# Neighbourhood and context probabilities as half-precision planes transposed by DMA, in a two-layer hybrid attention kernel on one core

## The chip, the core and the metric

The kernel runs on one core of one Trainium2 chip. The metric is the device time of one execution in microseconds (us), as the median over several runs. A core has a matrix engine (TensorE, "PE" in the profile, with its weight loads as "PEld"), a vector engine (VectorE, "DVE"), a scalar engine (ScalarE, "ACT"), a general one (GpSimd, "POOL") and a queue engine (SyncE, "SP") that here only issues DMA transfers. Each engine runs its own instructions in the order of its program and waits on semaphores. Sixteen DMA engines move data between memories.

## The reference

Two layers of a diffusion backbone. Each layer modulates and normalises 512 latent and 256 context tokens of width 1024, projects them once to the queries, keys, values and gates of two token mixers, and merges these. Mixer A is neighbourhood attention on an 8 x 64 grid with 8 heads of 64 (a window of 8 x 16 and a learned bias), whose latent queries also read all context keys. Mixer B is grouped-query attention, 8 query heads on 2 key heads. In the first layer the context is updated too, and its queries read only context keys.

```python
def _na_latent(q, k, v, kc, vc, rpb, rows):
    ...
        s_win = jnp.einsum('bchd,bicjhd->bhcij', qr, kw).astype(jnp.float32) * scale + bias[None]
        s_ctx = jnp.einsum('bchd,blhd->bhcl', qr, kc).astype(jnp.float32) * scale
        s = jnp.concatenate([s_win.reshape(B, NA_HEADS, GRID_W, wr * WIN_C), s_ctx], axis=-1)
        p = jax.nn.softmax(s, axis=-1).astype(v.dtype)
        ...
        return (jnp.einsum('bhcij,bicjhd->bchd', p_win, vw)
                + jnp.einsum('bhcl,blhd->bchd', p_ctx, vc))
...
def _layer(x, ctx, ...):
    hx = _rmsnorm(x, norm_g) * (1.0 + scale_x) + shift_x
    hc = _rmsnorm(ctx, norm_g) * (1.0 + scale_c) + shift_c
    px = hx @ w_in
    a_k, a_v, b_k, b_v, a_q, b_q, a_z, b_z, g_a, g_b = _split(px, SPLIT_SIZES)
    ...
    a_att = _na_latent(qa, ka, va, cka, cva, rpb, rows)
    ...
    b_att = _gqa_latent(qb, k_all, v_all)
    out_x = _merge(a_att, b_att, a_z, b_z, g_a, g_b, w_o_a, w_o_b, w_out)
    x_new = x + gate_x * out_x
    if update_ctx:
        c_a_att = _attend(cqa, cka, cva).reshape(B, L, NA_WIDTH)
        ...
        ctx = ctx + gate_c * out_c
    return x_new, ctx
```

## The kernel before

All is computed to single precision. Each large product is made of three products of split operands: a rounded high part (a 32-bit type with fewer mantissa bits, written `R(...)` in the code) and the remainder, `hi*hi + hi*lo + lo*hi` (`mm3`, L427 to L431). A weight tile is loaded from DRAM on SP's queue (`raw`, three buffers), rounded by ACT (`whi`), and its remainder is taken by DVE or POOL (`wlo`; L391 to L418).

A layer runs in stages. The latent and context rows are projected to keys, values and queries of mixer A; then comes the neighbourhood stage; then the projections of mixer B; then the grouped-query stage; then the output projections. In both attention stages `pipeline` (L993) goes over the eight heads: scores of head h, then the values of head h - 1, then a share of `fill`, which holds matmuls of other projections (gates and output) together with their weight loads. So TensorE has work beside the attention. The order in which each engine's program stands is made by a scheduler at build time; it may move instructions among one another within their dependences.

The neighbourhood stage, per head:

- `na_scores` (L934): four query blocks of 128. Block 0 holds the two edges of the grid, 64 queries each; blocks 1 to 3 hold the rest. Scores go to PSUM (L857, L858, L951), DVE adds the bias table and finds the maximum (L954), ACT takes the exponential and the sum (L957) into a tile `p` of 128 queries x 512 keys in 32 bits. `softmax_tail` (L756) normalises `p`: on DVE for blocks 0 and 2 (L761), on POOL for 1 and 3 (L763, L764). The bias tables `bint` and `bedg` have one buffer each and are loaded per head (L928).
- `ctx_scores` (L863), in layer 0 alone: 256 context queries on 256 context keys, in two blocks of 128.
- `na_values` (L964): `transpose_split` (L767) transposes 128x128 blocks of `p` on TensorE into PSUM (L773, L775), four blocks a call and four calls a head; ACT rounds the result to `pth` (L781) and DVE takes the remainder `ptl` (L782). Then TensorE multiplies them with the values, kept in two tiles `va` as high and low parts (L977 to L988). `ctx_values` (L884) does the same with one call for the context (L896 to L902).
- `head_out` (L785) adds the two halves of the result and multiplies it into `za`, the gate path's tile.

The grouped-query stage already has another form. Its probabilities are not normalised at first; `turned` (L795) writes them as two planes of 16-bit floats, ACT the rounded plane (L798) and DVE or POOL the remainder (L799), and a transposing DMA, issued on SP, writes them into `ht` (L800). `gq_values` (L1133) multiplies `ht` with values that are scaled to use the range of 16-bit floats (`shrink`, L811, and `split_vb`, L1068), as a high and a low part (and the high part once more), and `divide` (L802) applies the sums and the scale afterwards. The context's probabilities of this stage take the same way into `ct` (in the profile also under the name `vb`, the tile whose spare columns hold every other one).

The adaptive gates: `ada_steps` (L276) computes dot products on DVE in the background of other stages; at their end `ada_gate` (L310) writes 16 (layer 0) or 8 (layer 1) rows of 128 factors to DRAM (`gd`), straight from a tile that holds them as 128 rows of 16 or 8 (L317). They are read back, spread over all partitions, before the last projection (`gv`, L1180).

Large tiles of 128 x 3072 words come from a pool of nine (`big`, L89).

```python
pt = psw(512, "s" if att["spare"] and att["turn"] % 2 else "t")
...
        T.transpose(pt[:, c0:c0 + 128], src, ident)
...
S.copy(hi[:, n0:n1], pt[:, n0:n1])
V.tensor_tensor(lo[:, n0:n1], pt[:, n0:n1], F(hi[:, n0:n1]), ALU.subtract)
```

Of the kernel before, what the change touches and what calls it, by code (L numbers as in the profile page):

```python
# [25 lines left out]
NP_NA = (7, 8)  # L26
# [3 lines left out]
NT_NA = 2  # L30
# [20 lines left out]
def R(ap):  # L51
    return ap.bitcast(F32R)
# [18 lines left out]
def hybrid_kernel(es: ExitStack, tc, x, ctx, cvec, w_ada, w_ada0, small, gvec, w_in, w_o_a, w_o_b, w_out,  # L71
# [238 lines left out]
    def ada_gate(l, nv):  # L310
# [6 lines left out]
        nc.sync.dma_start(gd[l][0:n].rearrange("n p -> p n"), g[:, 0:nv].rearrange("p v k -> p (v k)"))  # L317
# [232 lines left out]
    def split_v(ps, hi, lo, hi_src=None):  # L550
        S.copy(R(hi), ps)
        V.tensor_tensor(R(lo), ps, hi, ALU.subtract)

    def evac_va(dsts):
        def f(t, ps):
            d = dsts[t // 3].rearrange("p (t n) -> p t n", t=3)[:, t % 3, :]
            d = d.rearrange("p (r q d) -> p r q d", q=4, d=64)
            s = ps.rearrange("p (r e d) -> p r e d", e=2, d=64)
            hi, lo = d[:, :, 0:4:3, :], d[:, :, 1:3, :]
            split_v(s, hi, lo)  # L560
        return f
# [18 lines left out]
    def layer(l, hx, nxt, start):  # L580
# [8 lines left out]
        def gate_steps(halves, pool):  # L589
            return (ada_steps(l, range(16, 24), halves, nv, pool)  # L590
                    + ([lambda: ada_gate(l, nv)] if 1 in halves else []))
# [133 lines left out]
        va = [big("va0"), big("va1")]  # L725
        w = load_w(W, C_AV, 512, KT, mix_lo)
        for t in range(6):
            tok_proj(w, 512, a_hx, t, evac_va(va))
# [26 lines left out]
        if True:  # L755
            def softmax_tail(p, n, r, pieces, eng=None):  # L756

                V.reciprocal(r, r)
                for i, (c0, c1) in enumerate(pieces):
                    if eng is None:  # L760
                        V.tensor_scalar(p[:, c0:c1], p[:, c0:c1], r[:, i:i + 1], 0.5, ALU.mult, ALU.mult)  # L761
                    else:
                        G.tensor_scalar(r[:, i:i + 1], r[:, i:i + 1], 0.5, None, ALU.mult)  # L763
                        G.tensor_tensor(p[:, c0:c1], p[:, c0:c1],  # L764
                                        r[:, i:i + 1].to_broadcast([128, c1 - c0]), ALU.mult)

            def transpose_split(blocks, n0=0, n1=512):  # L767

                att["turn"] += 1
                pt = psw(512, "s" if att["spare"] and att["turn"] % 2 else "t")  # L770
                for src, c0 in blocks:
                    if c0 is None:
                        T.transpose(pt.rearrange("p (s n) -> p s n", n=64)[:, 0:8:7, :], src, ident)  # L773
                    else:
                        T.transpose(pt[:, c0:c0 + 128], src, ident)  # L775
                if att["spare"]:
                    hi, lo = R(p_tile()[:, 0:512]), R(p_tile()[:, 0:512])
                else:
                    hi = att["p"].tile([128, 512], F32R, tag="pth", name=nm("pth"), bufs=att["nt"])
                    lo = att["p"].tile([128, 512], F32R, tag="ptl", name=nm("ptl"), bufs=att["nt"])  # L780
                S.copy(hi[:, n0:n1], pt[:, n0:n1])  # L781
                V.tensor_tensor(lo[:, n0:n1], pt[:, n0:n1], F(hi[:, n0:n1]), ALU.subtract)  # L782
                return hi, lo

            def head_out(po, e, dst, eng=None):  # L785
# [5 lines left out]
                S.copy(a, po[o:o + 64, :n])  # L791
                V.tensor_tensor(a, po[m:m + 64, :n], a, ALU.add)
                (eng or G).tensor_tensor(dst, dst, a, ALU.mult)

            def turned(p, n, out, eng):  # L795

                h = att["p"].tile([128, 2, n], F16, tag="h", name=nm("h"), bufs=att["nh"])
                S.copy(h[:, 0], p[:, :n])  # L798
                eng.tensor_tensor(h[:, 1], p[:, :n], h[:, 0], ALU.subtract)  # L799
                nc.sync.dma_start_transpose(out, h.rearrange("p a n -> p (a n)"))  # L800
# [9 lines left out]

            def shrink(v, s, mx, row):  # L811

                V.tensor_reduce(mx[:, 0:1], v, AX, ALU.max)
                V.tensor_reduce(mx[:, 1:2], v, AX, ALU.min, negate=True)
                V.tensor_tensor(mx[:, 0:1], mx[:, 0:1], mx[:, 1:2], ALU.max)
                pt = psw(512, "t")
                T.transpose(pt[0:1, 0:128], mx[:, 0:1], ident)
                V.tensor_reduce(row[:, 0:1], pt[0:1, 0:128], AX, ALU.max)
                T.matmul(pt[:, 128:129], row[:, 0:1].to_broadcast([1, 128]), ident[0:1, 0:1], start=True, stop=True)
                V.tensor_scalar(s[:, 1:2], pt[:, 128:129], 1.0e-30, 1.0 / V_UP, ALU.max, ALU.mult)  # L820
                V.reciprocal(s[:, 0:1], s[:, 1:2])
                V.tensor_scalar(s[:, 1:2], s[:, 1:2], 0.5, None, ALU.mult)
# [673 lines left out]
```

## Time and profile before

| | |
|---|---|
| median of 3 runs | 1131.86 us (1130.71 to 1135.87) |
| the profiled execution | 1136.54 us, span 1134.8 us, granted clock 0.989 |
| neighbourhood stage, layer 0 | about 150 to 305 us |
| grouped-query stage, layer 0 | about 384 to 507 us |
| neighbourhood stage, layer 1 | about 783 to 893 us |
| grouped-query stage, layer 1 | about 955 to 1066 us |
| DMA moved | 161.29 MB in 195278 packets |

All lines are of one profiled execution; times are from its first instruction. "Busy" of PE is modelled, since matmuls overlap: the start times in the timeline tell what one costs. In a group's row stand the line of the code, the engine, the operation, the tiles (out<-in), shape and count, then busy us and mean ns, then the idle time of the engine just before and what ended it. A row of a source line has the least, median and largest duration in ns. In the timeline a row has start, duration, engine (SPq: the queue of SP), line, operation and tiles; the idle time before it and its releaser stand in brackets.

### The profile page before, as it was taken

Reading aid. Unit: us, or ns where it says so; the run is one execution under the profiler, and the core shown is the slowest. Engines: PE = TensorE matmul, PEld = TensorE weight load, DVE = VectorE, ACT = ScalarE, POOL = GpSimd, SP = SyncE. Lnnn points to the kernel's source line nnn. Section 1 sums busy time; section 2 is a strip of 40 time slices with the busy share of each in tenths; the row PEclk is TensorE's granted clock in tenths of the full one; section 3 lists DMA queues with packets and bytes.
Section 4 is the critical chain, followed back from the end, with each engine's and each line's share of the span. In section 5 each row is a group of like instructions: output and inputs, shape, how many; then the busy total and the mean of one; then the engine's idle time right before and its main releaser. Section 6 shows DMA issues by size and latency. Waiting matters only on the chain.

```text
span 1134.8 us, 16867 instructions
## 1 busy us (share of the span) xinstructions
PE 1092.4 (96%) x5824; PEld 905.5 (80%) x5824; DVE 765.3 (67%) x1492; ACT 578.0 (51%) x1152; POOL 490.5 (43%) x405
## 2 busy tenths in 40 slices
PE   8999999999999999779999999999999999999998
PEld 5688888888988877557788888887888987777677
DVE  4666788888365478636567895357988765677473
ACT  6463266656333566555331275325666545776431
POOL 1044255654246245345521454335554563463530
PEclk9999999999999999989999999999999999999999
DMA  9454412233341597679733542453333236989742
GB/s 366 148 173 134 126 49 66 83 125 98 110 140 47 130 205 176 108 216 248 192 104 127 158 149 77 142 182 72 108 105 112 64 103 164 186 219 250 198 147 81
DMA packets 195278, 161.29 MB, mean 142 GB/s; under 512 B 119444, under 2 KB 161144, under 8 KB 193528
## 3 DMA queue, kind: packets, MB, share of 16 engines
q1 hardware_dynamic: 187856, 145.82, 47.2%
q0 software_dynamic: 2368, 7.87, 2.1%
q10 hardware_dynamic: 4968, 6.53, 1.7%
q8 instruction: 46, 0.75, 0.3%
q14 instruction: 40, 0.33, 0.1%
HBM read 115.58 MB, written 17.32 MB: 117 GB/s over the span
## 4 chain that ended last, share of the span: by engine, by line
PE 78%; DMA 6%; DVE 5%; issue 5%; POOL 3%; ACT 2%; SPq 1%; POOLq 0%; ACTq 0%; DVEq 0%
PE psx L431 11%; PE psx L430 11%; PE psx L429 11%; PE psf L429 9%; PE psf L430 8%; PE psf L431 8%; PE pst L775 2%; PE pss L951 2%; PE pss L857 2%; PE pss L858 2%; DMA raw<-in_w_in_dram 2%; DMA ht<-h 1%; PE pst L521 1%; PE pst L1144 1%; PE pst L1145 1%
## 5 line engine op out<-in xcount | busy, mean ns | idle before, releaser
L429 PE MATMUL psf<-hx,whi 128*128 128x512 f32 (+1 forms) x360 | 137.9, 383 | 4.1 <-ACT zt L610 2.5
L416 POOL TENSOR_TENSOR wlo<-raw,whi 128x512 fp32r<-128x512 f32 x70 | 98.0, 1405 | 94.4 <-ACT whi L414 64.3
L431 PE MATMUL psf<-hx,wlo 128*128 128x512 f32 (+1 forms) x360 | 135.8, 377 | 0.0
L430 PE MATMUL psf<-hx,whi 128*128 128x512 f32 (+1 forms) x360 | 135.2, 376 | 0.0
L429 PE MATMUL psx<-whi,hx 128*128 128x512 f32 (+1 forms) x328 | 120.7, 371 | 0.0
L430 PE MATMUL psx<-wlo,hx 128*128 128x512 f32 (+1 forms) x328 | 119.7, 366 | 0.0
L431 PE MATMUL psx<-whi,hx 128*128 128x512 f32 (+1 forms) x328 | 119.5, 365 | 0.0
L414 ACT CAST whi<-raw 128x512 fp32r<-128x512 f32 x136 | 82.5, 620 | 72.6 <-DMA raw<-in_w_in_dram 44.9
L402 POOL TENSOR_TENSOR wlo<-raw,whi 128x512 fp32r<-128x512 f32 x40 | 61.0, 1528 | 120.6 <-ACT whi L399 73.0
L799 POOL TENSOR_TENSOR h<-p,h 128x768 f16<-128x768 f32 (+1 forms) x40 | 64.9, 1626 | 99.7 <-ACT h L798 79.1
L399 ACT CAST whi<-raw 128x512 fp32r<-128x512 f32 x88 | 54.4, 623 | 100.4 <-PE psx L431 33.9
L500 POOL TENSOR_TENSOR ss<-ss,ehalf 128x8 f32<-128x8 f32 (+2 forms) x40 | 62.2, 1558 | 74.1 <-DVE ss L497 74.0
L416 DVE TENSOR_TENSOR wlo<-raw,whi 128x512 fp32r<-128x512 f32 x66 | 66.6, 1009 | 28.9 <-ACT whi L414 27.4
L1127 DVE CUSTOM_DVE_ANT_0 p<-pss,vb 128x768 f32<-128x768 f32 x64 | 60.2, 953 | 36.7 <-PE pss L858 19.9
L429 PEld LDWEIGHTS psf<-hx,whi 128*128 128x128 f32 x360 | 67.9, 189 | 16.1 <-ACT zt L610 3.6
L431 PEld LDWEIGHTS psf<-hx,wlo 128*128 128x128 f32 x360 | 67.8, 188 | 11.5
L430 PEld LDWEIGHTS psf<-hx,whi 128*128 128x128 f32 x360 | 67.9, 189 | 10.3
L1128 ACT ACTIVATE p<-pss,mx 128x768 f32<-128x768 f32 x64 | 57.5, 900 | 35.0 <-DVE mx L1127 31.5
L431 PEld LDWEIGHTS psx<-whi,hx 128*128 128x128 f32 x328 | 61.9, 189 | 10.0
L430 PEld LDWEIGHTS psx<-wlo,hx 128*128 128x128 f32 x328 | 62.0, 189 | 9.2
L429 PEld LDWEIGHTS psx<-whi,hx 128*128 128x128 f32 x328 | 61.7, 189 | 8.9
L429 PE MATMUL psx<-hx,whi 128*128 128x256 f32 (+1 forms) x208 | 68.1, 327 | 0.0
(359 smaller groups left out, 3097.5 us busy)
## 6 DMA issues: line engine op xcount, KB each, us to landing
raw<-in_w_in_dram SPq DMA_DIRECT2D x168, 256.0 KB, 2.9
rawb<-in_w_ada_dram SPq DMA_DIRECT2D x48, 256.0 KB, 2.8
raw<-in_w_out_dram SPq DMA_DIRECT2D x32, 256.0 KB, 3.1
tg<-gs SPq DMA_DIRECT2D x4, 1536.0 KB, 6.4
rawx<-in_w_ada_dram SPq DMA_DIRECT2D x4, 1024.0 KB, 13.3
rawy<-in_w_ada_dram SPq DMA_DIRECT2D x4, 1024.0 KB, 10.3
gs<-zt ACTq DMA_DIRECT2D x16, 256.0 KB, 2.1
raw<-in_w_o_a_dram SPq DMA_DIRECT2D x16, 256.0 KB, 3.4
```

The lines of the kernel that those rows point to most:

```text
L399: S.copy(hi[:, :n], raw[:, :n])
L402: e.tensor_tensor(lo[:, :n], raw[:, :n], F(hi[:, :n]), ALU.subtract)
L414: S.copy(hi, raw)
L416: lo_eng(i).tensor_tensor(lo, raw, F(hi), ALU.subtract)
L429: T.matmul(ps, lhs[0], rhs[0], start=first, stop=False)
L430: T.matmul(ps, lhs[0], rhs[1], start=False, stop=False)
L431: T.matmul(ps, lhs[1], rhs[0], start=False, stop=last)
L500: G.tensor_tensor(ss, ss, ehalf[:, :n], ALU.pow)
L775: T.transpose(pt[:, c0:c0 + 128], src, ident)
L799: eng.tensor_tensor(h[:, 1], p[:, :n], h[:, 0], ALU.subtract)
L1127: V.tensor_tensor_reduce(p, pss, lift, -1.0, 3e38, ALU.add, ALU.min, mx[:, 0:1])
L1128: S.activation(p, pss, AF.Exp, bias=mx[:, 0:1], accum_out=r[:, i:i + 1])
```

## The change

In the neighbourhood stage the probabilities too go through `turned` and a transposing DMA. `turned` gets the sums `r`: it forms the reciprocal, times 2^14, and on DVE's blocks (0 and 2) applies it while it writes the two 16-bit planes (ACT the rounded one, DVE the remainder in one fused operation); on POOL's blocks (1 and 3) POOL multiplies `p` by it first, ACT rounds and POOL takes the remainder. The DMA writes 128 transposed columns of `ht` per block; block 0 goes as two DMAs of 64 partitions each, to the two edges. The context's probabilities of layer 0 go the same way, one DMA a head, with DVE for the remainder.

The values `va` become pairs of 16-bit floats, scaled by the largest value over all tokens: each token tile is copied in 32 bits (`vf`), ACT takes absolute values and DVE their maximum (`size`), and after the first query tile `split_va` finds the largest over the partitions (a transpose and a small matmul on TensorE) and writes the pairs in three steps. The scale is taken back in `head_out`. The values of mixer B are held as pairs too, without the second high part. `transpose_split` and `softmax_tail` are gone.

`na_values` has four matmuls of 512 columns, four of 192 and eight of 128 per head, all on 16-bit operands; the two middle token tiles, which were one range of 256 columns, are now two of 128, since each query block's columns lie in their own plane. In `ctx_values` four of 256 columns stay.

`ht` has two places: part of one more large tile (`spare`) for even heads, a tile of the stage's pool for odd ones; `spare` holds the context's planes too. The number of `p` tiles goes from 7 and 8 to 3 and 4 (layers 0 and 1), `h` tiles are 3 and 4; tiles `r` go from 8 to 4.

`ada_gate` transposes its tile on TensorE, copies the rows out of PSUM on ACT and stores them as rows.

Instruction counts of the program: matmuls and transposes 5764 to 5546, transposing DMAs 72 to 160, other DMAs on SP 411 in both, POOL's two-operand operations 328 to 360, those of DVE 564 to 454.

```diff
-NP_NA = (7, 8)
+NP_NA = (3, 4)
+NH_NA = (3, 4)
-NT_NA = 2
+P_UP = 2.0 ** 14
...
-        nc.sync.dma_start(gd[l][0:n].rearrange("n p -> p n"), g[:, 0:nv].rearrange("p v k -> p (v k)"))
+        pt = psw(512, "t")
+        T.transpose(pt[0:n, 0:128], g[:, 0:nv].rearrange("p v k -> p (v k)"), ident)
+        gt = pool.tile([16, 128], F32, tag="agt", name=nm("agt"), bufs=1)
+        S.copy(gt[0:n], pt[0:n, 0:128])
+        nc.sync.dma_start(gd[l][0:n], gt[0:n])
...
+    def size(v, junk, mx):
+
+        S.activation(junk, v, AF.Abs)
+        V.tensor_reduce(mx, junk, AX, ALU.max)
+
+    def halves(v, d, s):
+
+        S.activation(d[:, :, 0, :], v, AF.Copy, scale=s)
+        V.scalar_tensor_tensor(d[:, :, 1, :], v, s, d[:, :, 0, :], ALU.mult, ALU.subtract)
...
+        def evac_va(t, ps):
+            S.copy(vf[:, t, :], ps)
+            size(ps, vab[:, 512 * t:512 * t + 512], vmx[:, t:t + 1])
+
+        def split_va():
+            V.tensor_reduce(vmx[:, 6:7], vmx[:, 0:6], AX, ALU.max)
+            shrink(vmx[:, 6:7], vsa, vsa[0:1, 2:3], 0.5 / P_UP)
+            for t in range(0, 6, 2):
+                halves(vf[:, t:t + 2, :].rearrange("p t (h d) -> p (t h) d", d=64),
+                       va[:, t:t + 2].rearrange("p t h q d -> p (t h) q d"), vsa[:, 0:1])
...
             tok_proj(w, 512, a_hx, t, evac_na(qav, True, gq, YB if first else 4))
+            if t == 0:
+                split_va()
...
-            def turned(p, n, out, eng):
+            def turned(p, n, out, eng, r=None):
 
                 h = att["p"].tile([128, 2, n], F16, tag="h", name=nm("h"), bufs=att["nh"])
-                S.copy(h[:, 0], p[:, :n])
-                eng.tensor_tensor(h[:, 1], p[:, :n], h[:, 0], ALU.subtract)
-                nc.sync.dma_start_transpose(out, h.rearrange("p a n -> p (a n)"))
+                if r is not None:
+                    V.reciprocal(r, r)
+                    eng.tensor_scalar(r, r, P_UP, None, ALU.mult)
+                    w = n // r.shape[-1]
+                if r is None or eng is G:
+                    if r is not None:
+                        G.tensor_tensor(p, p, r.to_broadcast([128, n]), ALU.mult)
+                    S.copy(h[:, 0], p[:, :n])
+                    eng.tensor_tensor(h[:, 1], p[:, :n], h[:, 0], ALU.subtract)
+                else:
+                    for i in range(n // w):
+                        c = slice(w * i, w * i + w)
+                        S.activation(h[:, 0, c], p[:, c], AF.Copy, scale=r[:, i:i + 1])
+                        V.scalar_tensor_tensor(h[:, 1, c], p[:, c], r[:, i:i + 1], h[:, 0, c], ALU.mult, ALU.subtract)
+                for o, (n0, n1) in out:
+                    nc.sync.dma_start_transpose(o, h[n0:n1].rearrange("p a n -> p (a n)"))
...
-                    softmax_tail(p, 512, r[:, 0:1], [(0, 512)], G if i in NA_POOL else None)
-                    ps_.append(p)
+                    at = [(0, 64, 0), (448, 512, 64)] if i == 0 else [(128 * i - 64, 128 * i + 64, 0)]
+                    turned(p, 512, [(ht[:, :, a:b], (n, n + b - a)) for a, b, n in at],
+                           G if i in NA_POOL else V, r[:, 0:1])
...
-                po = psw(512, "s" if h == 6 else "v")
+                    return va[:, t, h].rearrange("p q d -> p (q d)")
+                po = psw(512, "t")
                 for k in range(2):
...
-                    T.matmul(po, vsl(4 + k), hi, start=k == 0, stop=False)
-                    T.matmul(po, vsl(4 + k), lo, start=False, stop=False)
...
+                    for a in range(2):
+                        T.matmul(po, vsl(4 + k), ht[:, 4 * a + 2 + k, :], start=k + a == 0, stop=False)
+                for t, part in enumerate((((0, 192, 0),), ((64, 192, 1), (192, 320, 0)),
+                                          ((192, 320, 1), (320, 448, 0)), ((320, 512, 1),))):
+                    for n0, n1, k in part:
+                        for a in range(2):
+                            T.matmul(po[:, n0:n1], vsl(t), ht[:, 4 * a + k, n0:n1], start=False,
+                                     stop=t == 3 and a == 1)
```

More of the change, by code (lines that the diff above doesn't have):

```diff
@@ L755, in layer, with head_out @@
         if True:
[L756 to L785, printed above, removed]
+            def head_out(po, e, dst, eng=None, back=None):
                 n = dst.shape[-1]
@@ L1018, in na_first, with values_of @@
                 q = stage_q(qav[:, j, :], e)
[L1019 to L1022 removed]
+                st = na_scores(h, q, kh, kl)
+                if not first:
+                    return st, None
+                o = 4096 + 1024 * (h % 2)
+                ct = spare[:, o:o + 1024].rearrange("p (a i k n) -> p a i k n", a=2, i=2, k=2)
+                return st, ctx_scores(q, kh, kl, ct, False)
+            def values_of(dst, f, back, late):
                 def g(h, st):
```

158 lines of the change are left out of this document (61 added, 97 removed).

## The prediction

> **What bounds the kernel now.** I read the page's header first, then the busy time of each engine by stage, then the instruction timeline of TensorE around every hole, then the timeline of SP's queue.
>
> ```profile
> span 1134.8 us, 16867 instructions
> PE 1092.4 (96%) x5824; PEld 905.5 (80%) x5824; DVE 765.3 (67%) x1492; ACT 578.0 (51%) x1152; POOL 490.5 (43%) x405
> ```
>
> TensorE has no holes for 96% of the span, so its work is the time, plus its few holes. By stage (columns: stretch, its length, busy us of PE, weight loads, DVE, ACT, POOL, then granted clock, DMA share, GB/s; the rows are neighbourhood attention of layer 0, grouped-query attention of layer 0, and the same two of layer 1):
>
> ```profile
> 150.00:305.00 155.00, 155.00 (x971) 138.38 (x970) 121.36 (x272) 93.02 (x212) 75.29 (x74) 1.00 0.28 87
> 384.00:507.00 123.00, 104.23 (x601) 84.72 (x599) 81.78 (x154) 77.67 (x151) 49.54 (x36) 0.96 0.78 165
> 783.00:893.00 110.00, 108.54 (x598) 93.24 (x599) 92.97 (x186) 73.94 (x155) 57.66 (x56) 1.00 0.34 102
> 955.00:1066.00 111.00, 105.31 (x499) 79.43 (x498) 77.23 (x122) 77.33 (x138) 61.29 (x42) 1.00 0.98 219
> ```
>
> Both neighbourhood stages are bound by TensorE alone, with the DMA engines two thirds idle. The grouped-query stages already transpose by DMA: there the DMA share is 0.78 and 0.98, and TensorE is idle 18.8 and 5.7 us. Most of the 18.8 is one hole:
>
> ```profile
> 486.71 0.59 PE L1144 MATMUL pst<-ht,vb 128*128 128x512 f16 x1 [11.83 <-DMA ht<-h]
> 489.60 0.38 PE L1145 MATMUL pst<-ht,vb 128*128 128x512 f16 x1
> ...
> 464.93 0.37 SPq L317 DMA_DIRECT2D gd<-ag  x1
> ...
> 467.89 16.43 SPq L800 DMA_TRANSPOSE ht<-h  x3
> ...
> 468.00:476.00 8.00, 6.88 (x48) 6.22 (x46) 6.71 (x12) 4.42 (x10) 2.89 (x3) 1.00 0.18 9
> 480.00:488.00 8.00, 1.29 (x4) 0.49 (x5) 1.93 (x3) 4.34 (x8) 1.54 (x2) 0.50 1.08 234
> ```
>
> The gate store at 464.93 writes 2048 separate 4-byte values. Behind it SP's queue stands: three transposes take 16.43 us to issue, the DMA engines move 9 GB/s for 8 us, and TensorE waits 11.83 us for a transposed tile. The clock then stands at 0.50.
>
> **1. Transposes leave TensorE.** By the code a head has 16 transposes of 128x128 (L773, L775), and in layer 0 four more for the context: 16 x 16 + 8 x 4 = 288.
>
> ```profile
> L775 PE MATMUL pst<-ident,p 128*128 128x128 f32 x212 | 35.3, 272 | 0.0
> L773 PE MATMUL pst<-ident,p 128*128 128x128 f32 x60 | 16.0, 272 | 0.0
> ...
> 183.83 0.27 PE L773 MATMUL pst<-ident,p 128*128 128x128 f32 x1
> 183.93 0.49 PE L775 MATMUL pst<-ident,p 128*128 128x128 f32 x3
> 184.26 0.27 PE L773 MATMUL pst<-ident,p 128*128 128x128 f32 x1
> 184.37 0.49 PE L775 MATMUL pst<-ident,p 128*128 128x128 f32 x3
> 184.62 0.47 PE L429 MATMUL psf<-hx,whi 128*128 128x512 f32 x1
> 184.93 0.39 PE L430 MATMUL psf<-hx,whi 128*128 128x512 f32 x1
> 185.16 0.40 PE L431 MATMUL psf<-hx,wlo 128*128 128x512 f32 x1
> ```
>
> One lasts 272 ns, but they overlap: four go from 183.83 to 184.26, so 0.11 us each from start to start. The next four and a 512-column matmul take 0.67 us up to 184.93, and that matmul alone 0.23 (184.93 to 185.16): again 0.11. I take the spacing: 288 x 0.11 = 31.7 us off the path.
>
> The Trainium skill ("TensorE: Matmul & The Clock Gate", Part 4: PE-mode transpose) puts a transpose at about 275 ns in a kernel. The duration here agrees; by it the gain would be 79 us, but the start times decide.
>
> **2. Value matmuls.** Before, a head has four of 512 columns at 0.23, then eight of 192 or 256. After, four of 512, four of 192 and eight of 128, in half precision.
>
> ```profile
> 1013.76 0.38 PE L1145 MATMUL pst<-ht,vb 128*128 128x512 f16 x1
> 1013.98 0.38 PE L1144 MATMUL pst<-ht,vb 128*128 128x512 f16 x1
> ...
> 156.84 0.22 PE L857 MATMUL pss<-kh,qs 128*128 128x128 f32 x1
> 156.90 0.28 PE L858 MATMUL pss<-kl,qs 128*128 128x128 f32 x1
> 157.02 0.39 PE L857 MATMUL pss<-kh,qs 128*128 128x384 f32 x1
> ```
>
> Half precision goes at 0.22 per 512 columns. By columns alone a head takes 4 x 0.22 + 4 x 0.083 + 8 x 0.055 = 1.65 us after, and 4 x 0.23 + 4 x 0.086 + 4 x 0.115 = 1.72 before. But the second 128-column matmul above takes 0.12 to the next one's start (156.90 to 157.02), the first 0.06. At 0.12 for all eight a head takes 2.17. So -1 to +7 us over 16 heads; I take 0, since the two rows lie on both sides of 0.055 to 0.12. The largest value of V and the gate rows add, over both layers, four transposes and two tiny matmuls: 0.6 us, 1 with their waits (bounds 0 and 3); projection matmuls stand around each and hide them, and without that cover each shows its DVE reduction, about 0.7.
>
> **3. The gate store.** Rows go out as 16 descriptors of 512 bytes. In layer 0 this gives back the hole and the slow clock after it: seven matmuls go from 486.71 to 489.60 in 2.9 us instead of 7 x 0.22, 1.4 us more. 11.8 + 1.4 = 13.2 us. In layer 1 the same store holds weight loads:
>
> ```profile
> 767.69 0.38 SPq L317 DMA_DIRECT2D gd<-ag  x1
> ...
> 772.23 12.04 SPq L411 DMA_DIRECT2D raw<-in_w_in_dram  x4
> ...
> 784.02 0.50 PE L429 MATMUL psf<-hx,whi 128*128 128x512 f32 x1 [1.61 <-DVE za L612]
> ```
>
> There 1.6 us, bounds 0 and 2. What is late next is what is late already: of layer 0's 18.8 us without the 11.8, 7 us are other small holes, and I leave them as they are.
>
> **4. What it adds to DMA and SP.** Per head three full transposes (128x1024) and two of 64 partitions; in layer 0 one more for the context. That is 88 more issues on SP, whose queue also carries weight loads and bias tables.
>
> ```profile
> L800 SPq DMA_TRANSPOSE ht<-h x64: 1273/1594/12456, 388.6 to 1060.1; - x64
> L800 SPq DMA_TRANSPOSE ct<-h x4: 1232/1426/2273, 418.4 to 551.0; - x4
> ht<-h SPq DMA_TRANSPOSE x64, 4.3
> ...
> 789.94 0.89 SPq L411 DMA_DIRECT2D raw<-in_w_in_dram  x2
> 791.01 0.34 SPq L929 DMA_DIRECT2D bint<-in_bias_int_dram  x1
> 791.62 1.11 SPq L931 DMA_DIRECT2D bedg<-in_bias_edge_dram  x2
> ...
> 871.25 0.38 SPq L929 DMA_DIRECT2D bint<-in_bias_int_dram  x1
> ```
>
> Engine time: layer 1's two attention stages have similar loads, and 32 transposes of 128x1536 lift the share from 0.34 of 110 us to 0.98 of 111. So (108.8 - 37.4) / 32 = 2.2 us each, 1.5 for 128x1024. Four equivalents a head in layer 1 add 48 us to 37: 85 of some 95 us, 0.9. Layer 0: five a head, 60 + 43 = 103 of some 137, 0.75.
>
> Queue time in layer 1: a head lasts (871.25 - 791.01) / 6 = 13.4 us; without its transposes 11.6. SP issues five transposes at 1.43 or less (7.1), bias 1.45, four weight loads at 0.45 (1.8) and a spill taken at the bias load's 0.34: 10.7 of 11.6 us. That is tight. In the changed program's order TensorE reads a head's transposed tiles only after the next head's scores, about a head of matmuls later, so some 11 us cover the 4.3 us landing. The bias table has one buffer: SP waits for a head's last score row before it reloads it, and the transposes and weight loads stand behind that wait; before, only weight loads did. If the queue slips further, the cover is gone: each late weight load holds ACT's rounding, then POOL's remainder, then TensorE.
>
> **5. Vector engines.**
>
> ```profile
> L782 DVE TENSOR_TENSOR ptl<-pst,pth 128x512 fp32r<-128x512 f32 x35 | 23.5, 682 | 3.2 <-ACT pth L781 3.0
> L761 DVE TENSOR_SCALAR p<-p,r 128x512 f32<-128x512 f32 x32 | 23.8, 744 | 0.7
> L1074 DVE SCALAR_TENSOR_TENSOR vb<-vf,vb 128x768 f16<-128x768 f32 x2 | 2.4, 1224 | 1.7 <-ACT vb L1072 1.7
> L799 POOL TENSOR_TENSOR h<-p,h 128x512 f16<-128x512 f32 x8 | 9.8, 1219 | 16.3 <-ACT h L798 11.6 <-issue 4.7
> ```
>
> DVE loses four subtractions (2.6) and two scalings (1.5) a head and gains two fused ones at 1224 x 512/768 = 0.82, two tiny ones: -2 us a head. POOL gains two subtractions, 2.4 us a head: in layer 1 57.7 + 19.5 = 77 of 95. ACT stays, save six absolute values and three wide roundings of V per layer, hidden by the projections' matmuls (uncovered, the last three with their remainders are 3 x 1224 x 1024/768 = 4.9 us a layer). All of it hides while TensorE runs, but layer 1 then has every engine and the DMA at 0.8 to 0.9. For new waits, bounds from the stages above: none (layer 0's neighbourhood stage now has 155.00 of 155), or two to three times what the grouped-query stage shows (5.7 us idle of 111 at share 0.98). I take 3 us in layer 0 (0 to 15) and 8 in layer 1 (0 to 20), nearer the grouped-query row as share and chain are alike.
>
> **Sum.** -31.7 + 0 + 1 - 13.2 - 1.6 + 11 = -34.5 us against the profiled execution, whose own time is 1136.54 (span 1134.8 and 1.7 around it), 4.7 above the median of 1131.86. 1131.9 - 34.5 = 1097 us.
>
> **Rivals.**
>
> A (0.61): as summed, from 1085 (no new wait, value matmuls at -1) to 1110 (25 us of waits and slow small matmuls).
>
> B (0.19): the transposing queue sets layer 1's pace. Then its neighbourhood stage keeps its 110 us, losing its 14 us of the 31.7, and layer 0 loses half of its 17.6: 1131.9 - 14.8 - 8.8 + 1 = 1109, to 1128 where layer 0 and the small matmuls give back more. For: 0.98 share in its twin. Against: TensorE still ran 105 of 111 there. The Trainium skill ("DMA: Bandwidth & Descriptors", Specifications) wants 512 bytes or more for line rate, which speaks against many small transposing packets; the 0.98 share at 219 GB/s agrees.
>
> C (0.07), slower: every head exposes one transpose to TensorE, because its remainder comes last on POOL and SP then takes it behind weight loads whose buffer is not free. Price: issue 1.6 + landing 4.3 = 5.9 us, 16 heads, 94 us against the 46.5 won: 1131.9 + 1 + 94 - 46.5 = 1180. It decides from 2.9 us a head. Against: the head of matmuls in between, by the order above.
>
> D (0.10): the store is not what stands in SP's queue; the hole comes back behind other transposes: 1097 + 13 = 1110.
>
> E (0.03): transposes cost TensorE their whole 272 ns: 47 us more, 1050.
>
> **Numbers.** Forecast 1097. The range 1083 to 1123 holds A, D and most of B; it leaves out C, E and B's end. No change means within 0.5% (5.7 us), about what a measurement can tell. Faster takes A, D, E and B but its end: 0.88; same 0.05; slower 0.07.
>
> **What would show it.** TensorE's records fall by some 220 and spacing elsewhere stays; no hole over 3 us near the gate store, whose followers issue in about 1.5 us; neighbourhood stages near 140 and 100 us, DMA shares near 0.75 and 0.9. Holes at the value matmuls waiting for ht say C; at weight rounding waiting for raw loads, B. Wrong altogether if either neighbourhood stage is longer than now.

## The result: slightly slower, and the profile after

| | before | after |
|---|---|---|
| median | 1132.52 us (1130.71 to 1135.87, 7 runs) | 1138.45 us (1136.35 to 1139.72, 7 runs) |
| ratio to before, 95% interval | | 1.0049 [1.0036, 1.0062] |
| the profiled execution, its span, granted clock | 1136.54, 1134.8, 0.989 | 1139.45, 1137.6, 0.980 |

The forecast was 1097 us; the change costs 5.9 us instead, 0.5%, with an interval that is clear of no change. The head of the page after:

```profile
span 1137.6 us, 16739 instructions
PE 1075.8 (95%) x5608; PEld 872.4 (77%) x5608; DVE 780.9 (69%) x1472; ACT 603.7 (53%) x1180; POOL 535.1 (47%) x437
```

TensorE has 216 records fewer, as foreseen, yet DVE and POOL are both busier than before. By stage (same columns as in the prediction: stretch, length, busy us of PE, weight loads, DVE, ACT, POOL, then clock, DMA share, GB/s; neighbourhood and grouped-query stage of layer 0, then of layer 1):

```profile
150.00:302.00 152.00, 136.90 (x790) 113.14 (x789) 126.32 (x254) 100.22 (x216) 96.03 (x89) 0.94 0.69 151
407.00:555.00 148.00, 131.18 (x719) 102.18 (x720) 102.95 (x177) 90.02 (x173) 68.25 (x50) 0.97 0.84 193
790.00:898.00 108.00, 96.56 (x494) 75.75 (x493) 84.31 (x164) 73.01 (x146) 78.50 (x70) 0.94 0.78 176
973.00:1073.00 100.00, 95.69 (x454) 70.20 (x452) 66.94 (x107) 67.42 (x120) 57.63 (x39) 1.00 0.92 218
```

Layer 0's neighbourhood stage had TensorE busy for 155.00 of 155 us; now it is idle for 15.1 of 152, with a granted clock of 0.94. The stages' lengths alone mislead: the scheduler moved projection matmuls out of the neighbourhood stages into the stretches behind them. So I compare each stage with the TensorE work that lies in it, and for the stages before I take the stretches that hold the same part of the program. They differ from the prediction's in two places (layer 0's grouped-query and layer 1's neighbourhood stage, before):

```profile
401.00:558.00 157.00, 134.04 (x730) 105.78 (x731) 98.81 (x179) 89.86 (x174) 68.98 (x50) 0.93 0.78 182
779.00:891.00 112.00, 110.00 (x599) 93.85 (x597) 94.42 (x186) 73.80 (x153) 57.97 (x57) 1.00 0.35 105
```

Work is the number of matmuls of each shape times the spacing at which that shape starts when nothing holds it (0.2275 us for 512 columns in 32 bits, 0.2165 in 16 bits, and so on); *lost* is the rest of the stage. It holds idle time and slow clock, and the choice of the spacings moves it by about 1 us a stage.

| lost, us | before | after |
|---|---|---|
| neighbourhood, layer 0 | 1.2 | 26.0 |
| grouped query, layer 0 | 31.8 | 23.9 |
| neighbourhood, layer 1 | 4.2 | 20.4 |
| all else | 26 | 28 |
| whole span | 63 | 98 |
| TensorE work in the whole span | 1072 | 1040 |

The work fell by 32 us, which the prediction had as 31.7. Counted without these spacings, as TensorE's busy time less half of what lay at half clock, it fell from 1085.1 to 1058.6 us, so by 26.5. The losses rose by 35. So the gain was earned and given back in the two neighbourhood stages, +25 and +16. What TensorE waited for there, after (engine, tile and line, releaser: us in total, times, longest; layer 0 first, then layer 1):

```profile
PE pst L971 <- DMA ht<-h: 4.0, 4, 1.3
PE psv L894 <- DMA ht<-h: 3.5, 2, 1.9
PE psv L894 <- DVE r L803: 3.0, 1, 3.0
PE psf L434 <- DVE zt L624: 2.2, 2, 1.8
...
PE pss L861 <- DVE mx L951: 5.4, 3, 2.3
PE psx L434 <- DVE mx L951: 2.9, 1, 2.9
PE pss L948 <- DVE mx L951: 2.1, 2, 1.5
```

In layer 1 nearly all of it is DVE: mostly PSUM tiles of scores that DVE has not emptied yet. In layer 0 half is transposed tiles that land late, and these are written by DVE or POOL before the transfer.

**Why DVE is late.** Groups of instructions on DVE in layer 0's neighbourhood stage, first after, then before (out<-in, shape, count | busy us, mean ns | idle before):

```profile
L815 DVE SCALAR_TENSOR_TENSOR h<-p,r,h 128x256 f16<-128x256 f32 x16 | 18.2, 1173 | 4.1 <-DMA gs<-zt 2.2 <-ACT h L814 1.7
L951 DVE CUSTOM_DVE_ANT_0 p<-pss,bint 128x512 f32<-128x512 f32 x24 | 15.9, 682 | 0.3
L815 DVE SCALAR_TENSOR_TENSOR h<-p,r,h 128x512 f16<-128x512 f32 x16 | 15.2, 952 | 3.3 <-ACT h L814 3.2
L855 DVE TENSOR_TENSOR qs<-qa,qs 64x768 fp32r<-64x768 f32 x7 | 13.2, 1892 | 0.2
```

```profile
L954 DVE CUSTOM_DVE_ANT_0 p<-pss,bint 128x512 f32<-128x512 f32 x24 | 16.2, 683 | 2.7 <-PE pst L775 2.1 <-PE pst L773 0.2
L782 DVE TENSOR_TENSOR ptl<-pst,pth 128x512 fp32r<-128x512 f32 x21 | 14.3, 683 | 2.7 <-ACT pth L781 2.6
L851 DVE TENSOR_TENSOR qs<-qa,qs 64x768 fp32r<-64x768 f32 x7 | 9.9, 1413 | 1.3 <-ACT qs L850 1.2
```

The fused operation takes longer on 256 columns (1173 ns) than on 512 (952), which its own work can't explain; on 256 columns its least duration is 472 ns and its longest 4518. The same old instruction on a head's queries (`qs`) went from 1413 to 1892 ns. The bias addition, which reads its scores from PSUM, takes 682 and 683. The removed remainders, too, read from PSUM (683). The removed scalings of `p` worked on SBUF. So the change swapped DVE work that in good part reads PSUM for work that reads SBUF alone, and gave POOL a subtraction for each of its two blocks beside it (POOL 75.29 to 96.03 us in this stage). What happens then is plainest at one place of the grouped-query stage, after (timeline; start, duration, engine, line, idle time before in brackets):

```profile
496.68 1.27 POOL L421 TENSOR_TENSOR wlo<-raw,whi 128x512 fp32r<-128x512 f32 x1
497.90 7.14 POOL L665 TENSOR_TENSOR gal<-za,gah 128x768 fp32r<-128x768 f32 x4
504.98 1.29 POOL L421 TENSOR_TENSOR wlo<-raw,whi 128x512 fp32r<-128x512 f32 x1
...
498.55 8.27 DVE L421 TENSOR_TENSOR wlo<-raw,whi 128x512 fp32r<-128x512 f32 x1
506.85 0.95 DVE L855 TENSOR_TENSOR qs<-qb,qs 64x768 fp32r<-64x768 f32 x1
508.03 0.42 DVE L793 TENSOR_TENSOR ho<-psv,ho 64x256 f32<-64x256 f32 x1
...
501.32 0.42 PE L862 MATMUL pss<-gk,qs 128*128 128x256 f32 x1
508.50 0.69 PE L824 MATMUL psv<-ident,r 128*128 128x128 f32 x2 [6.76 <-DVE ho L793]
```

A weight remainder that DVE does elsewhere in 0.69 us starts at 498.55, while POOL runs one instruction after the other, and ends at 506.82, 0.55 us after POOL's run ends (504.98 + 1.29 = 506.27). Behind it wait a query's remainder, `head_out` and, for 6.76 us, TensorE. I call *stretch* what DVE's instructions of a stage last beyond the least duration that the same line has for the same shape anywhere in the run: 17.1 us before and 35.4 after in layer 0's neighbourhood stage, 21.8 and 27.1 in layer 1's. (The expectations below quote 32.5 and 16.6 for what is 35.4 and 21.1 by this count.) The Trainium skill ("SBUF — State Buffer", Who interferes with whom) has a DVE instruction with two SBUF inputs contend with a GpSimd instruction that reads SBUF. The rows agree: both kinds stand here side by side, and DVE's takes 8.27 us instead of 0.69.

**The gate store** no longer makes TensorE wait. SP's queue behind it in the timeline, then the windows of the same time, after:

```profile
478.77 0.85 SPq L322 DMA_DIRECT2D gd<-agt  x1
479.73 1.28 SPq L817 DMA_TRANSPOSE vb<-h  x1
481.63 7.88 SPq L817 DMA_TRANSPOSE ht<-h  x2
```

```profile
478.00:486.00 8.00, 8.00 (x43) 5.89 (x42) 4.32 (x9) 5.04 (x10) 2.88 (x3) 1.00 0.82 154
486.00:494.00 8.00, 8.00 (x48) 6.04 (x48) 4.05 (x8) 4.90 (x9) 2.16 (x3) 1.00 0.54 91
```

The first transpose behind it issues in 1.28 us; the next two still take 7.88 together, but the hole of 11.83 us is gone: TensorE is busy throughout. The hole of 6.76 us above now begins 23 us behind the store, at 501.74.

### The profile page after: what moved, and what is told of

Its sections match the earlier page's. It is cut to its first block, busy times and chain, and to the rows that moved or that the text cites. A ratio compares the mean times of both kernels' runs of the same rounds, so it can differ in the third digit from the quotient of the medians.

```text
span 1137.6 us, 16739 instructions
## 1 busy us (share of the span) xinstructions
PE 1075.8 (95%) x5608; PEld 872.4 (77%) x5608; DVE 780.9 (69%) x1472; ACT 603.7 (53%) x1180; POOL 535.1 (47%) x437
## 4 chain that ended last, share of the span: by engine, by line
PE 28%; DVE 7%; issue 6%; DMA 4%; POOL 4%; ACT 2%; SPq 0%; POOLq 0%; DVEq 0%; ACTq 0%
PE psx L436 5%; PE psx L434 5%; PE psx L435 5%; PE psf L434 3%; PE psf L435 3%; PE psf L436 3%; DMA raw<-in_w_in_dram 1%; DVE wlo L421 1%; DMA raw<-in_w_o_a_dram 1%; PE pst L1134 1%; PE pst L1135 1%; POOL wlo L407 1%; DMA ht<-h 1%; DMA rawb<-in_w_ada_dram 1%; PE pss L861 1%
## 5 line engine op out<-in xcount | busy, mean ns | idle before, releaser
L810 POOL TENSOR_TENSOR h<-p,h 128x512 f16<-128x512 f32 (+1 forms) x72 | 108.1, 1503 | 105.8 <-ACT h L809 81.7
L421 DVE TENSOR_TENSOR wlo<-raw,whi 128x512 fp32r<-128x512 f32 x66 | 74.8, 1134 | 42.1 <-ACT whi L419 39.8
L809 ACT CAST h<-p 128x768 f16<-128x768 f32 (+1 forms) x104 | 77.2, 748 | 27.9 <-POOL p L808 18.8
L435 PEld LDWEIGHTS psf<-hx,whi 128*128 128x128 f32 x360 | 68.9, 191 | 11.2
```

The source lines that it names most:

```text
L421: lo_eng(i).tensor_tensor(lo, raw, F(hi), ALU.subtract)
L435: T.matmul(ps, lhs[0], rhs[1], start=False, stop=False)
```

## Experiments

Each run's median stands against runs of the kernel before on the same chip (medians 1131.8 to 1133.2), the ratio with its 95% interval. Differences between medians of runs from different chips are therefore good to about 1 us. N0 and N1 are the us lost in the two neighbourhood stages, G0 in layer 0's grouped-query stage.

| run | median us | ratio | N0 | N1 | G0 |
|---|---|---|---|---|---|
| gates_only | 1127.21 | 0.9956 [0.9939, 0.9973] | 1.5 | 3.6 | 22.2 |
| gates_hilo | 1125.60 | 0.9932 [0.9917, 0.9946] | 1.2 | 3.8 | 15.9 |
| old_gate | 1142.17 | 1.0086 [1.0064, 1.0109] | 26.9 | 22.6 | 28.7 |
| bias2 | 1135.58 | 1.0038 [1.0015, 1.0062] | 25.9 | 19.1 | 23.7 |
| bufs | 1135.81 | 1.0033 [1.0012, 1.0054] | 26.4 | 20.3 | 23.2 |
| dve_probs | 1123.33 | 0.9923 [0.9901, 0.9945] | 15.5 | 16.0 | 22.1 |
| pool_load | 1144.73 | 1.0096 [1.0075, 1.0117] | 27.7 | 28.1 | 22.9 |
| no_turn | 1130.48 | 0.9967 [0.9956, 0.9978] | 22.1 | 9.2 | 22.5 |
| no_turn_dve | 1115.25 | 0.9844 [0.9829, 0.9858] | 13.7 | 8.0 | 22.7 |
| no_low | 1092.62 | 0.9654 [0.9636, 0.9672] | 2.7 | 1.2 | 22.4 |
| hilo_dve | 1121.29 | 0.9893 [0.9860, 0.9927] | 16.4 | 15.4 | 19.2 |
| combo | 1121.59 | 0.9892 [0.9874, 0.9910] | 16.2 | 13.7 | 16.9 |
| one_pool | 1120.97 | 0.9894 [0.9879, 0.9909] | 18.7 | 13.3 | 15.8 |
| relief | 1112.19 | 0.9829 [0.9802, 0.9856] | 11.2 | 10.7 | 16.3 |

In the three runs whose neighbourhood stages have no transposes (no_turn, no_turn_dve, no_low) layer 1's stage ends earlier in the program's order, so their N1 is not a like comparison; the stretch up to the grouped-query stage loses 10.3, 5.4 and 0.9 more.

**The gate rows, alone and undone.** gates_only is the kernel before with `ada_gate` as in the change; old_gate is the changed kernel with

```diff
-        pt = psw(512, "t")
-        T.transpose(pt[0:n, 0:128], g[:, 0:nv].rearrange("p v k -> p (v k)"), ident)
-        gt = pool.tile([16, 128], F32, tag="agt", name=nm("agt"), bufs=1)
-        S.copy(gt[0:n], pt[0:n, 0:128])
-        nc.sync.dma_start(gd[l][0:n], gt[0:n])
+        nc.sync.dma_start(gd[l][0:n].rearrange("n p -> p n"), g[:, 0:nv].rearrange("p v k -> p (v k)"))
```

> The kernel before with the gate rows alone (a transpose on TensorE, a copy on ACT, a store of whole rows). If the 4-byte store is what held SP's queue, the hole of 11.8 us in layer 0's grouped-query stage and the slow clock behind it go: 1132.5 - 13 to -15, 1118 to 1120 us. If another wait takes its place there (the changed kernel shows a new hole of 6.8 us at a DVE instruction that lasts 8.3 us), about 1125. If the store was not the cause, 1132.

> The changed kernel with the gates stored as before. The same three readings from the other side: 1138.5 + 13 to 15 = 1152 if the store costs all of its hole, about 1146 if another wait stands in for half of it, 1138 if it was not the cause.

The rows are worth 1133.2 - 1127.2 = 6.0 us alone and 1142.2 - 1138.5 = 3.7 beside the rest, both less than a whole hole; the rest of the change alone therefore costs 0.86% [0.64, 1.09]. In old_gate TensorE's longest wait in that stage is again one for a transposed tile, 8.7 us. The 12-us hole is gone in gates_only, but there too TensorE stands still for 6.9 us somewhat later. The timeline of gates_only there:

```profile
490.38 1.27 POOL L420 TENSOR_TENSOR wlo<-raw,whi 128x512 fp32r<-128x512 f32 x1
491.61 7.13 POOL L657 TENSOR_TENSOR gal<-za,gah 128x768 fp32r<-128x768 f32 x4
498.70 1.26 POOL L420 TENSOR_TENSOR wlo<-raw,whi 128x512 fp32r<-128x512 f32 x1
...
492.27 8.24 DVE L420 TENSOR_TENSOR wlo<-raw,whi 128x512 fp32r<-128x512 f32 x1
```

Again DVE's instruction ends 0.55 us after POOL's run (500.51 against 499.96).

**That hole taken away.** gates_hilo is gates_only with the four POOL remainders on DVE:

```diff
-            hilo(za, gated["a"], range(4))
+            hilo(za, gated["a"], range(4), V)
```

> The kernel before with the gates' factors stored as rows (gates_only, 1127.2 us) and, besides, the remainders of mixer A's gated tile taken by VectorE instead of GpSimd. Nothing is left out. Theory 1 (the 6.9 us hole in layer 0's grouped-query stage that stands in gates_only is a weight remainder on VectorE that waits out those four GpSimd remainders): the hole is gone or under 2 us, and the time falls to 1120 to 1124, near the 13 us of gain that the prediction gave the rows. Theory 2 (the hole has another cause, or VectorE is late itself with the four more operations): 1125 to 1129 with a hole of the same size.

The hole is gone; TensorE's longest wait in that stage is 1.6 us, and the stage loses 15.9 instead of 22.2, against 31.8 before: all of the predicted 13.2 and more. But the time falls by only 1.6 us, to 1125.6, above the 1120 to 1124 expected, and the two intervals overlap. The stretch from there to layer 1's neighbourhood stage loses 5.4 instead of 1.8. So the cause of the hole is shown, and also that most of what is won there is lost again, in part in that stretch; why stays open.

**The bias table and the number of tiles.** bias2 has two `bint` tiles, used in turn; bufs has more tiles for the probabilities.

```diff
-            bint = att["p"].tile([128, 512], F32, tag="bint", name=nm("bint"), bufs=1)
+            bints = [att["p"].tile([128, 512], F32, tag=f"bint{j}", name=nm("bint"), bufs=1) for j in range(2)]
...
-NP_NA = (3, 4)
-NH_NA = (3, 4)
+NP_NA = (4, 6)
+NH_NA = (3, 6)
```

> The changed kernel with two buffers for the interior bias table, so that SP need not wait for a head's last score row before it loads the next. If DVE's wait for that table (6.2 us in layer 1's neighbourhood stage) is on the path: 1138.5 - 3 to -8 us with the slow clock behind its holes, 1130 to 1135. If the wait only stands beside others: 1137 to 1139.

> The changed kernel with more tiles for the probabilities: p tiles 4 and 6 instead of 3 and 4, h tiles 3 and 6 instead of 3 and 4 (layers 0 and 1). Nothing is left out. Theory 1 (GpSimd and VectorE side by side cost the time): 1135 to 1140, as the tiles don't change who computes. Theory 2 (the cut in tiles from 7 and 8 holds the score rows, and so TensorE): 1120 to 1130, with TensorE's waits for score rows in layer 1 mostly gone.

Neither is the main cause: some 3 us each against 1138.5, with intervals that overlap that of the change, so that even these 3 us are not shown. In the changed kernel DVE does wait for the table in layer 1:

```profile
DVE p L951 <- DMA bint<-in_bias_int_dram: 6.2, 4, 2.7
```

In bias2 these waits are no longer in the list, but the stage loses 19.1 us instead of 20.4: DVE's time was short elsewhere as well.

**POOL's share of the probabilities on DVE.** In dve_probs no query block goes to POOL.

```diff
-NA_POOL = (1, 3)
+NA_POOL = ()
```

> The changed kernel with all four query blocks on ACT and DVE (none on POOL): POOL loses some 80 us over both layers, DVE gains 32 x 0.9 = 28 us. Theory 1, DVE's instructions with SBUF operands are stretched while POOL runs (the fused remainder takes 0.74 us alone and up to 4.5 us beside POOL), so DVE is late and TensorE waits for it: the stretched ones fall back to 0.74, the time falls by 10 to 25 us, to 1114 to 1128. Theory 2, transposes and SP's queue are late: within 4 us of 1138. Theory 3, DVE is simply too full: slower than 1140.

1138.5 to 1123.3: 15 us, though DVE has 32 fused operations more (16 in this stage) and POOL nothing of these probabilities. The groups of L815 and then the stage's window in dve_probs:

```profile
L815 DVE SCALAR_TENSOR_TENSOR h<-p,r,h 128x512 f16<-128x512 f32 x32 | 27.1, 854 | 5.0 <-ACT h L814 4.9
L815 DVE SCALAR_TENSOR_TENSOR h<-p,r,h 128x256 f16<-128x256 f32 x16 | 8.6, 564 | 0.7 <-ACT h L814 0.7
```

```profile
150.00:286.00 136.00, 126.49 (x764) 107.34 (x762) 120.85 (x285) 99.11 (x214) 53.52 (x41) 0.96 0.75 161
```

With POOL at 53.52 us instead of 96.03, the 256-column form takes 564 ns instead of 1173, and DVE does more in less time (120.85 against 126.32). The queries' instruction (`qs`) takes 1579 ns instead of 1892. The stretch falls from 35.4 to 21.1 us.

**Is it POOL's running, or POOL's place in the chain?** pool_load puts idle POOL work back into dve_probs: it writes a scratch tile that nothing reads.

```diff
+            scr = att["p"].tile([128, 512], F32, tag="scr", name=nm("scr"), bufs=1)
+            V.memset(scr, 0.0)
...
+                    if i in (1, 3):
+                        for _ in range(2):
+                            G.tensor_tensor(scr, scr, r[:, 0:1].to_broadcast([128, 512]), ALU.mult)
```

> The kernel with all of the neighbourhood probabilities on VectorE (dve_probs, 1123.3 us), to which idle work on GpSimd is added: for query blocks 1 and 3 of each head two multiplications of a 128x512 scratch tile by the block's scale, some 1.05 us each, 33 us in a stage; nothing reads the scratch tile. Nothing is left out. Theory 1 (VectorE's instructions wait while GpSimd runs, whatever GpSimd computes): VectorE's stretch in layer 0's neighbourhood stage goes from 16.6 us back towards the changed kernel's 32.5, and the time from 1123 to 1130 to 1138. Theory 2 (what cost the time was GpSimd's own latency inside the chain from probability to transposed tile): that chain doesn't hold the scratch work, so the time stays within 1120 to 1126 and the stretch below 20 us.

1123.3 to 1144.7 us, 21 us for work of which nothing is used, more than was expected. Its groups in layer 0's neighbourhood stage, and the only row under those that waited for the scratch line (who waited: us, times):

```profile
L815 DVE SCALAR_TENSOR_TENSOR h<-p,r,h 128x512 f16<-128x512 f32 x32 | 31.4, 994 | 2.1 <-ACT h L814 2.1
L953 DVE CUSTOM_DVE_ANT_0 p<-pss,bint 128x512 f32<-128x512 f32 x24 | 16.2, 679 | 0.1
L815 DVE SCALAR_TENSOR_TENSOR h<-p,r,h 128x256 f16<-128x256 f32 x16 | 15.3, 988 | 0.1
L963 POOL TENSOR_TENSOR scr<-scr,r 128x512 f32<-128x512 f32 x32 | 38.5, 1203 | 14.6 <-DVE r L804 7.0 <-DVE r L803 6.4
```

```profile
  ACT ho L795: 0.5, 1
```

The window of that stage, to be set beside that of dve_probs:

```profile
151.00:299.00 148.00, 129.50 (x763) 106.37 (x762) 134.85 (x285) 99.53 (x214) 96.33 (x73) 0.97 0.67 149
```

The fused operations are stretched again (994 and 988 ns), the operation on PSUM is not (679), and only once, for 0.5 us, does anything wait for the scratch work itself. DVE's same number of instructions (285) is busy for 134.85 us instead of 120.85, and the stretch is 34.4 us in layer 0's stage and 29.4 in layer 1's (21.1 and 16.5 in dve_probs). This settles that POOL's running costs DVE's time. It does not settle that all of the 21 us comes this way: POOL's useful work stands in line behind the scratch work, and ACT waits for that 7.4 us in layer 0's stage (3.0 in dve_probs), TensorE 1.6 in layer 1's.

**The transposing DMAs.** no_turn leaves out the 88 transposing DMAs of the neighbourhood stages (the planes of `ht` are zeros), so mixer A's neighbourhood attention and, in layer 0, its context attention are not computed. no_turn_dve does so in dve_probs.

```diff
-                for o, (n0, n1) in out:
+                for o, (n0, n1) in out if r is None else []:
```

> The changed kernel without the 88 transposing DMAs of the two neighbourhood stages; the transposed tiles are set to zero once per stage instead, so the neighbourhood and first-layer context attention of mixer A are left out of the result. All work of the engines stays. Theory 2 (late transposes and SP's queue cost a good part of the 46 us that TensorE loses in these stages): the holes at the value matmuls and at the bias table go, 10 to 20 us less, 1119 to 1128. Theory 1 (DVE beside POOL makes nearly all of them): 1133 to 1138.

> The same with all query blocks on ACT and DVE (against 1123.3 with the transposes; the same part of the result is left out). Theories 1 and 2 together: what is still lost there (15.5 and 16.0 us) falls below 8 each, 1108 to 1114. If the loss is instead the chain of DVE and ACT that each head needs, with less TensorE work around it: 1118 to 1123.

8.0 us in the one (1138.5 to 1130.5) and 8.1 in the other: that much is SP's queue, the landing and the DMA engines' load together. Both times lie between the ranges that the two theories gave. POOL's part is 15 us with and without them (1138.5 to 1123.3, 1130.5 to 1115.3), so the two add up. But with both gone the neighbourhood stages still lost far more than before.

**What was left.** no_low is no_turn_dve without the fused remainder (the low planes aren't computed either). relief is the full computation: combo with the keys' rounded copy on ACT.

```diff
-                        V.scalar_tensor_tensor(h[:, 1, c], p[:, c], r[:, i:i + 1], h[:, 0, c], ALU.mult, ALU.subtract)
...
-                V.tensor_copy(rows(kh, e), k)
+                S.copy(rows(kh, e), k)
```

> As no_turn_dve (1115.3 us; all neighbourhood probabilities on VectorE, no transposing DMAs in the neighbourhood stages), and besides the low half-precision planes of the neighbourhood and its context's probabilities aren't computed: 48 and 32 fused operations on VectorE fewer, some 39 and 27 us of its work in the two stages. Left out are the low planes and the transposes, so mixer A's neighbourhood attention and, in layer 0, its context attention. Theory 1 (VectorE's amount of work is what is left: 121 of 131 us busy): the stages lose 1 to 4 us each instead of 13.4 and 7.7, and the time falls to 1098 to 1105. Theory 2 (another thing holds TensorE: the bias table, the three PSUM tiles of the score rows, ScalarE's exponentials): 1110 to 1116, with the same waits.

> As combo (1121.6 us; all neighbourhood probabilities and the remainders of mixer A's gated tile on VectorE, two bias tables), and the rounded copy of each head's keys on ScalarE instead of VectorE: 0.55 to 1.2 us a head off VectorE, 0.83 more on ScalarE. Nothing is left out. Theory 1 (VectorE is the bound of layer 0's neighbourhood stage): 3 to 6 us less, 1115 to 1119. Theory 2 (VectorE isn't, or ScalarE's queue ahead of the exponentials is as tight): 1120 to 1125.

no_low's windows of the two neighbourhood stages, then relief's of layer 0's:

```profile
153.00:274.00 121.00, 120.01 (x744) 102.06 (x744) 88.73 (x237) 97.20 (x212) 50.71 (x41) 1.00 0.31 96
776.00:838.00 62.00, 62.00 (x332) 47.91 (x331) 48.28 (x147) 60.45 (x122) 28.52 (x19) 1.00 0.37 114
```

```profile
150.00:284.00 134.00, 125.53 (x770) 107.00 (x769) 117.29 (x279) 103.75 (x220) 50.81 (x40) 0.99 0.80 169
```

With DVE at 89 of 121 us, TensorE is idle for 1 us of 121 and the clock stays at 1.00; 22.6 us go with that one operation, more than the 10 to 17 expected. So DVE's amount of work is the rest. From the other side, moving a copy that in combo takes DVE 0.55 us a head in layer 0's stage (the group `kh<-ka`) to ACT wins 9 us (1121.6 to 1112.2), more than I expected.

**Versions on the way.** hilo_dve is dve_probs with `hilo` on DVE; combo adds the two bias tables; one_pool is hilo_dve with block 3 on POOL again.

> The kernel with all query blocks on ACT and DVE, and with the four remainders of mixer A's gated output (1.8 us each, back to back on POOL in layer 0's grouped-query stage) moved to DVE. There a DVE weight remainder lasts 8.3 us beside them and TensorE stands 5.8 to 6.9 us. Theory 1: the hole goes, 1123 - 5 to -9 us with the slow clock behind it: 1114 to 1118. If the hole belongs to the chain of that place whatever engine takes the remainders: 1122 to 1125.

> The same with two buffers for the interior bias table. If the effects add: the previous one - 2 to -4, 1111 to 1116; if the bias wait was covered once DVE is freer: no difference.

> All on VectorE but query block 3, which is GpSimd's again; the remainders of mixer A's gated tile on VectorE (hilo_dve, 1121.3 us). Nothing is left out. Theory 1 (each block on GpSimd costs by the stretch it puts on VectorE): half of the 15 us between blocks 1 and 3 on GpSimd and none, so 1127 to 1131. Theory 2 (VectorE, busy 121 of 136 us in layer 0's neighbourhood stage without GpSimd, is itself the bound by then, and one block on GpSimd relieves it): 1114 to 1120.

All three lie within 0.7 us of one another, 1.1% under the kernel before. hilo_dve is 2.0 us under dve_probs, whose interval overlaps its own. one_pool met neither of its expectations. Its stretch is 26.8 us in layer 0's neighbourhood stage, against 21.1 in dve_probs; that this and what the block takes off DVE cancel is likely but not shown. combo shows that a second bias table adds nothing here. relief, at 0.9829 [0.9802, 0.9856], is the fastest kernel of the study that computes everything.

## Why the prediction was wrong, step by step

**Part 1, transposes: right.** TensorE's work fell by 32 us by spacings and by 26.5 counted without them; the spacing of 0.11 us was about the right price, not the 0.27 us that one transpose lasts, which would have made it 78. Rival E falls.

**Part 2, value matmuls: right, on the lower bound.** A layer 0 head's values, after:

```profile
300.11 1.04 PE L971 MATMUL pst<-ht,va 128*128 128x512 f16 x4
300.98 0.94 PE L976 MATMUL pst<-ht,va 128*128 128x192 f16 x12
301.76 0.60 PE L894 MATMUL psv<-ht,va 128*128 128x256 f16 x4
```

300.11 to 301.76 is 1.65 us, the figure by columns alone; the small matmuls go at 0.056, not 0.12.

**Part 3, the gate store: mechanism right, size wrong.** -13.2 and -1.6 were taken; 6.0 alone and 3.7 in place were measured. What failed here is "What is late next is what is late already". What came next was a remainder on DVE behind POOL's run, hidden until then. Rival D was near, but the hole came back behind DVE, not behind other transposes. A part may also lie in the execution that was read, whose time was 4 us over the median; that is not shown.

**Part 4, DMA and queue: right.** Shares of 0.69 and 0.78 stand against 0.75 and 0.9, and the transposes cost 8 us, below the 11 that the sum allowed for all new waits. Rival B's mechanism is there with that price and does not set the pace; rival C's 94 us did not come.

**Part 5, vector engines: the step that failed.** It is "All of it hides while TensorE runs". With "-2 us a head", DVE was to have 121.4 - 16 = 105 us in layer 0's stage. Measured: 126.3. By least durations DVE's work did fall, from 104 to 91 us; of the 21 us of difference, 18 are the growth of the stretch, 35.4 - 17.1, for which the prediction had no term. The fused operation was priced at 0.82 us from two wide operations that stand elsewhere; beside POOL it took 0.95 on the mean, and 1.17 in the half-width form. So where TensorE's work fell to 126 us, DVE's time rose to 126: it became a second bound, and what was too late on DVE came out as new waits and slow clock. The bounds of these (0 to 15 and 0 to 20) came from layer 1's grouped-query stage, where only the DMA share and the chain were alike, and not DVE's share: 77.23 of 111 us there, against 126 of 152 here. Measured were +25, outside its bounds, and +16, inside but twice the 8 us taken.

**The sum again.** Against the forecast the neighbourhood stages' losses are 41 - 11 = 30 us off and the gate store 14.8 - 6.0 = 9 us: 39 of the 41 us by which the time was missed. The warning "wrong altogether if either neighbourhood stage is longer than now" did not ring: they were 3 and 4 us shorter, because the scheduler had moved projection work out of them. Two other signs did fail: the stages were not near 140 and 100 us, and a hole over 3 us stood behind the gate store.

## What to carry to other kernels

Before pricing an operation that moves to another engine, ask where its operands lie: here DVE work that reads its scores from PSUM ran beside POOL untouched (679 to 683 ns throughout), and a fused operation on SBUF took twice as long on the mean (1173 ns against 564). When TensorE loses work, compare what is left with each other engine's busy time in that stage, stretched as it will be there, because the next engine becomes the bound as soon as the two meet. When a hole is closed, look in the trace for the next instruction that was late under its cover, and size the gain up to there.

## What the runs showed of the hardware that I had not expected

DVE's wait beside POOL is not that for one instruction. An instruction of 0.69 us lasted 8.27 us in the changed kernel and 8.24 in gates_only, through five POOL instructions in a row, and ended 0.55 us after the last of them both times. The Trainium skill ("SBUF — State Buffer", Summary: rules for kernel authors) has the second of the two block until the first finishes; read by itself, that would be a wait for one POOL instruction.

The clock can halve after holes of under 2 us. After (timeline of TensorE, then the window in which the clock is slow):

```profile
196.25 0.50 PE L434 MATMUL psf<-hx,whi 128*128 128x512 f32 x1 [1.85 <-DVE zt L624]
...
198.00 0.63 PE L434 MATMUL psf<-hx,whi 128*128 128x512 f32 x1
198.42 0.63 PE L435 MATMUL psf<-hx,whi 128*128 128x512 f32 x1
```

```profile
198.00:200.00 2.00, 2.00 (x6) 1.62 (x5) 1.94 (x6) 0.13 (x1) 1.76 (x3) 0.50 0.41 93
```

The last hole before it is 1.85 us long, and then a 512-column matmul starts every 0.42 us instead of 0.23. The Trainium skill ("TensorE: Matmul & The Clock Gate", Part 1, What's actually happening) gives at least one idle window of some 3.4 us for this. Here no single hole in the 12 us before was longer than 1.93 us. The half clock lasted 17 us in layer 0's neighbourhood stage and 14 in layer 1's, and none before, which is part of what was lost there.
